# Five groups' expert results by way of DRAM, in a mixer and mixture-of-experts block

## The chip, the cores and the metric

One core of one Trainium2 chip runs the whole program. The metric is the device time in microseconds (us) from start to end of one execution, taken as the median of three runs. The profile shows one further execution of the same program.

## The reference

The block has three stages. RMSNorm and modulation of 512 latent and 256 context tokens of 1,024 elements feed a combined projection, two bidirectional linear recurrences (GLA and retention), a gated merge and an output projection. Then comes the part that the change touches, a hierarchical mixture of experts, and at the end a final RMSNorm:

```python
def hier_moe(h, w_rg, b_rg, w_re, b_re, w_gate, w_up, w_down):
    # top-1 of 4 groups, then top-2 of the 8 experts in it: 512 tokens x 2 = 1,024 rows over 32 experts
    ...
    x_pad = jnp.zeros((P, D), h.dtype).at[dest].set(xt[stok])
    ...
    def expert_block(args):
        xb, e = args
        hid = jax.nn.silu(xb @ w_gate[e]) * (xb @ w_up[e])
        return hid @ w_down[e]
    y = lax.map(expert_block, ...)
    out = jnp.zeros((T, D), jnp.float32).at[tok_pad].add(y.astype(jnp.float32) * w_pad[:, None])

h_lat = h_lat + g2 * hier_moe(modulate(rmsnorm(h_lat, norm_ffn), sh2, sc2), ...)
return rmsnorm(h_lat, norm_final)
```

Everything is fp32. Each expert has a gate, an up (1,024 x 256) and a down matrix (256 x 1,024), 3.1 MB together, about 100 MB for all 32.

## The kernel before

Tokens are put into slots: 14 groups of 128 slots, and each group serves one, two or four experts (2, 2, 4, 1, 4, 1, 2, 4, 1, 2, 4, 1, 2, 2 of them). Which experts share a group follows from how many tokens each one has. The first two groups hold experts whose weights are loaded before the routing is known. `tokG` holds each slot's token, `slotw` its routing weight, `slot` each token's two slot numbers, and `hres[0..3]` the residual stream, 128 tokens each.

Weights come as 192 tiles of 128 x 1,024 (0.5 MB each) in the order of the list `TL`; `feed` (L1108) issues them on SyncE's queue, gate and up at L1124, down at L1127, into a ring of 34 buffers `raw` (L1098). A buffer is handed on when TensorE's matmuls on it are issued (`done_with`). The framework gives each DMA issue one of eight semaphores in turn, in the order of the program text, and an issue waits until the DMA that had its semaphore before has landed.

For each group the main loop (L1476) runs `tokens` (gather of token rows by Pool, transposes on TensorE L1145), `gate_up` (L1158, both products into one PSUM tile, then SiLU on ACT and a product on VectorE), `hidden` (transposes L1174) and `down` in two halves k = 0, 1 (L1185). After the second half `add_results` (L1199) weights the result (`y`, VectorE, L1205), splits it into two parts of reduced precision (`yh` on ACT L1206, `yl` on VectorE L1207), builds a one-hot matrix of the slots' tokens (`hot`, L1209) and appends eight "units" to a list: a unit is two matmuls that spread 128 slots over 128 tokens (L1215) and a VectorE add into `hres` (L1216). The next group's `gate_up` works the units off between its own matmuls, in portions of 0, 2, 3 and 3; what is left is done at the start of the next `add_results`. `y`, `yh` and `yl` have one buffer each. Pools of named tiles, with waits set by the framework, keep everything in order; on each engine instructions run in the order that the framework's scheduler has written.

After the last group `results` (L1427) squares and normalises `hres` and stores the four output tiles (L1438). The routing ahead of the stage (L847 to L893) modulates each 128 tokens on Pool and ACT (L863, L866, L868) and stores them to DRAM as `xf_d`, from which the gathers (L984) read.

Of the kernel before, what the change touches and what calls it, by code (L numbers as in the profile page):

```python
# [11 lines left out]
F32 = mybir.dt.float32  # L12
F32R = mybir.dt.float32r
I32 = mybir.dt.int32
# [28 lines left out]

NE = 11
NR = 8
NB = 8
NL = 7
RING = NE + NR + NB + NL

# [9 lines left out]
NG = len(GROUPS)  # L59

GIVE = (0, 2, 3, 3)
LC = 3
LRJ = 5
PUMP = 5
# [60 lines left out]
def kernel(ctx: ExitStack, tc: tile.TileContext, io, dbg=None):  # L125
# [21 lines left out]
    def pj(shape=(128, 512)):  # L147
        return ps.tile(list(shape), F32, name="pj", bufs=4)
# [655 lines left out]
            feat_block(io[wb][0], 256 * j, (Branch(br, 0), Branch(br, 1)), False, merge(br, j))  # L804


    xf_d = dram.tile([T, D], F32, name="xf_d")

    wr = sb.tile([128, NK, 40], F32, name="wr")
# [145 lines left out]
    tokF, slotw = (sb.tile([128, NG], F32, name=n) for n in ("tokF", "slotw"))  # L955
    ctl = sb.tile([1, 32], I32, name="ctl")
    slot = sb.tile([128, 4, 2], F32, name="slot")
    capr = sb.tile([128, 32], F32, name="capr")
    bno = sb.tile([128, 1], F32, name="bno")
    nc.gpsimd.memset(bno, 0.0)  # L960
# [6 lines left out]
    def ring(kind, n, size, make):  # L967

        r = RINGS.setdefault(kind, {})
        if n % size not in r:  # L970
            r[n % size] = make()
        return r[n % size]

    def w4(name, dt=F32):
        return PM[0].tile([128, D], dt, name=name, tag="w4", bufs=8)
# [78 lines left out]
    def slot_weights():  # L1054

        w, P = RK["ing"], RK["P"]
        nc.vector.tensor_mul(w, w, wk.rearrange("p i k -> p (i k)")[:, :, None].to_broadcast([128, 8, NG]))
        pw = sc((128, NG))
        for m in range(8):
            nc.tensor.matmul(pw, P[:, m].bitcast(F32), w[:, m], start=(m == 0), stop=(m == 7))  # L1060
        nc.vector.tensor_copy(slotw, pw)

    def overflow():

# [114 lines left out]
    def down(g, k):  # L1179
        st, (kind, *es) = EX[g], GROUPS[g]  # L1180
        if k == 0:
            st["p"] = pj(), pj()
        for n2 in range(2):
            for e, r in zip(es, halves(g)):
                nc.tensor.matmul(st["p"][n2][r], st["h"][:, k, r], WT["d", g, k, 0, e][:, 512 * n2:512 * (n2 + 1)],  # L1185
                                 start=(k == 0), stop=(k == 1))
        done_with(len(es))
        if k == 0:
            return
        y, h, l = (ring(n, 0, 1, lambda: w4(n, F32 if n == "y" else F32R)) for n in ("y", "yh", "yl"))  # L1190
        add_results(st["p"], slotw[:, g:g + 1], tokF[:, g:g + 1], y, h, l, one_hot(g % 2))
        del EX[g]

    def one_hot(n):
        if not HT:
            HT[0] = t4([128, 2, 4, 128], "hot", F32R)
        return HT[0][:, n]

    def add_results(p, w, tok, y, h, l, hot):  # L1199

        while units:
            units.pop(0)()
        for n2 in range(2):
            cs = slice(512 * n2, 512 * (n2 + 1))
            nc.vector.scalar_tensor_tensor(y[:, cs], p[n2], w, ada_b[3][:, cs], op0=OP.mult, op1=OP.mult)  # L1205
            nc.scalar.copy(h[:, cs], y[:, cs])  # L1206
            nc.vector.tensor_sub(l[:, cs], y[:, cs], h[:, cs])  # L1207
        for i in range(4):
            nc.vector.tensor_scalar(hot[:, i], iot, 128.0 * i, tok, op0=OP.add, op1=OP.is_equal)  # L1209

        def unit(i, n):
            cs = slice(512 * n, 512 * (n + 1))
            q = sc()
            for m, x in enumerate((h, l)):
                nc.tensor.matmul(q, hot[:, i], x[:, cs], start=(m == 0), stop=(m == 1))  # L1215
            nc.vector.tensor_add(hres[i][:, cs], hres[i][:, cs], q)  # L1216

        units.extend(partial(unit, i, n) for i in range(4) for n in range(2))

    raws, staged = {}, {}  # L1220
# [122 lines left out]
    def overflow_block(po):  # L1343

        def t4(shape, name, dt=F32):
            big = math.prod(shape[1:]) == D
            return po.tile(shape, dt, name=name, tag="b4" if big else name, bufs=6 if big else 1)
# [67 lines left out]
        for n2 in range(2):  # L1415
# [4 lines left out]
            for k in range(2):  # L1420
                nc.tensor.matmul(p, hT[:, k], w[:, k], start=(k == 0), stop=(k == 1))
            ps2.append(p)
        add_results(ps2, ow, otok, t4([128, D], "y"), t4([128, D], "yh", F32R), t4([128, D], "yl", F32R), one_hot(0))
        while units:
            units.pop(0)()

# [49 lines left out]
    for g in range(NG + 1):  # L1476
        early = g == len(PAIR_EARLY)
        if early:
            down(g - 1, 0)
            down(g - 1, 1)  # L1480
        if g < NG:
            gate_up(g)
            if g + 2 < NG:
                tokens(g + 2)
        if g and not early:
            down(g - 1, 0)
        if g < NG:
            hidden(g)
        if g and not early:
            down(g - 1, 1)  # L1490
        if g == 0:
            slot_weights()
        if g == 3:
            extra = overflow()
        if g == NG - 1:

            free = -(-(len(TL) - NE - NR - NB) // RING) * RING + NE + NR + NB
            nfin = raw_tile(free)
            nc.sync.dma_start(nfin, bass.AP(tensor=io["norm_final"].tensor, offset=io["norm_final"].offset,
                                            ap=[[0, 128], [1, D]]))  # L1500

            with tc.issue_after(last["hT"].ins):
                nc.scalar.activation(small(1, "va"), eps, AF.Sqrt)
# [31 lines left out]
```

## Time and profile before

| | |
|---|---|
| time, median of 3 runs | 1128.74 us (1125.59 to 1130.0) |
| profiled execution, own time | 1129.64 us |
| its span | 1127.8 us |
| TensorE busy | 1026.6 us (91%) |
| VectorE, ACT, Pool busy | 609.4 (54%), 344.1 (31%), 262.6 us (23%) |
| granted TensorE clock, mean | 0.963 of full speed |
| read from DRAM, written | 188.44 MB, 4.19 MB |
| share of the chain that ended last | TensorE 50%, VectorE 5%, DMA 1% |

The page cuts the span into 40 slices of 28.2 us. The expert stage takes the last ten, from about 846 us:

```profile
PE   3989899899999999999999999999729999999993
...
DMA  9860212332223302433442251448179999999801
GB/s 304 207 206 20 67 38 85 94 96 54 76 64 106 112 26 72 140 102 79 129 149 75 75 168 56 131 146 339 48 264 385 407 407 408 407 408 407 329 1 76
```

In the first two rows a digit is the busy share of a slice in tenths; the third is what the DMA engines moved. TensorE is busy in both long stages; the DMA engines are full in the expert stage alone.

### The profile page before, as it was taken

How to read it: one execution, taken by the hardware profiler on the slowest of the kernel's cores; microseconds unless marked ns; L12 is line 12 of the kernel's file. 1: busy time of each engine (PE TensorE's matmuls, PEld its weight loads, DVE VectorE, ACT ScalarE, POOL GpSimd, SP SyncE). 2: the span in 40 equal slices, each digit the busy share in tenths (PEclk: the TensorE clock that was granted, in tenths of full speed). 3: DMA queues.
4: the chain of work that ended last, by engine and by line, in shares of the span. 5: the costliest groups of instructions: out<-in, count | busy, mean ns of one | idle time of the engine just before them, and what ended most of it. 6: DMA issues, size and time to landing. Idle time of an engine off the chain costs nothing.

```text
span 1127.8 us, 17400 instructions
## 1 busy us (share of the span) xinstructions
PE 1026.6 (91%) x6726; PEld 837.9 (74%) x6726; DVE 609.4 (54%) x1113; ACT 344.1 (31%) x594; POOL 262.6 (23%) x316
## 2 busy tenths in 40 slices
PE   3989899899999999999999999999729999999993
PEld 1779888799898988999887888889726655554542
DVE  4546677877688444534544241463352655454556
ACT  4237345455443222122233132333321111111012
POOL 0014234443726142414230100121431000000001
PEclk9999899999999999999999999999759999999997
DMA  9860212332223302433442251448179999999801
GB/s 304 207 206 20 67 38 85 94 96 54 76 64 106 112 26 72 140 102 79 129 149 75 75 168 56 131 146 339 48 264 385 407 407 408 407 408 407 329 1 76
DMA packets 105773, 190.66 MB, mean 169 GB/s; under 512 B 10882, under 2 KB 72660, under 8 KB 105688
## 3 DMA queue, kind: packets, MB, share of 16 engines
q1 hardware_dynamic: 98968, 180.53, 46.9%
q10 hardware_dynamic: 4576, 4.78, 1.4%
q0 software_dynamic: 2144, 4.21, 1.0%
q8 instruction: 54, 0.88, 0.3%
q14 instruction: 31, 0.25, 0.1%
HBM read 188.44 MB, written 4.19 MB: 171 GB/s over the span
## 4 chain that ended last, share of the span: by engine, by line
PE 50%; DVE 5%; DMA 1%; issue 1%; ACT 1%; POOL 0%; SPq 0%; ACTq 0%; DVEq 0%; POOLq 0%
PE pj L341 16%; PE pj L1158 10%; PE pj L332 9%; PE sc L1215 5%; PE pj L1185 4%; PE sc L1145 1%; DMA xg<-xf_d,tokG 1%; DVE y L1205 1%; PE sc L862 1%; DVE hres L1216 1%; DVE wl L1243 0%; DVE qs L594 0%; PE sc L1174 0%; ACT yh L1206 0%; PE sc L755 0%
## 5 line engine op out<-in xcount | busy, mean ns | idle before, releaser
L332 PE MATMUL pj<-wh,xh 128*128 128x256 f32 x800 | 229.7, 287 | 3.6 <-ACT wh L1238 2.3
L332 PE MATMUL pj<-wh,xl 128*128 128x256 f32 x800 | 227.4, 284 | 0.0
L332 PE MATMUL pj<-wl,xh 128*128 128x256 f32 x800 | 227.1, 284 | 0.0
L1243 DVE TENSOR_TENSOR wl<-raw,wh 128x1024 fp32r<-128x1024 f32 x88 | 118.6, 1355 | 100.6 <-ACT wh L1238 53.2
L332 PEld LDWEIGHTS pj<-wh,xh 128*128 128x128 f32 x800 | 153.9, 192 | 4.7 <-ACT wh L1238 2.5
L332 PEld LDWEIGHTS pj<-wh,xl 128*128 128x128 f32 x800 | 153.0, 191 | 0.7
L332 PEld LDWEIGHTS pj<-wl,xh 128*128 128x128 f32 x800 | 152.4, 191 | 0.2
L1238 ACT CAST wh<-raw 128x1024 fp32r<-128x1024 f32 x88 | 91.5, 1048 | 170.0 <-PE pj L332 44.2
L1158 PE MATMUL pj<-raw,xt 128*32 128x256 f32 (+2 forms) x1024 | 118.2, 383 | 0.0
L1158 PEld LDWEIGHTS pj<-raw,xt 128*32 128x32 f32 (+2 forms) x1024 | 69.6, 130 | 40.3 <-issue 9.6
L1216 DVE TENSOR_TENSOR hres<-hres,sc 128x512 f32<-128x512 f32 x112 | 71.0, 683 | 39.6 <-PE sc L1215 39.6
L341 PE MATMUL pj<-xh,wh 128*128 128x512 f32 (+1 forms) x216 | 82.8, 388 | 3.3 <-ACT wh L1238 3.2
L341 PE MATMUL pj<-xl,wh 128*128 128x512 f32 (+1 forms) x216 | 82.8, 385 | 0.0
L341 PE MATMUL pj<-xh,wl 128*128 128x512 f32 (+1 forms) x216 | 82.5, 382 | 0.0
L341 PE MATMUL pj<-oT,wh 128*128 128x512 f32 x256 | 81.7, 399 | 0.8 <-ACT oT L760 0.5
L703 DVE SCALAR_TENSOR_TENSOR adaacc<-wada,scT,adaacc 128x1024 f32<-128x1024 f32 x28 | 39.3, 1403 | 41.9 <-DMA wada<-in_w_ada 41.9
L1215 PE MATMUL sc<-yh,hot 128*128 128x512 f32 x112 | 50.4, 457 | 9.4 <-ACT yh L1206 9.0
L341 PEld LDWEIGHTS pj<-oT,wh 128*128 128x128 f32 x256 | 48.2, 191 | 12.6 <-ACT oT L760 1.0
L1185 PE MATMUL pj<-raw,hT 128*32 128x512 f32 (+2 forms) x256 | 53.6, 600 | 0.0
L341 PE MATMUL pj<-oT,wl 128*128 128x512 f32 x128 | 50.3, 395 | 0.0
L1215 PE MATMUL sc<-yl,hot 128*128 128x512 f32 x112 | 47.9, 437 | 2.5 <-DVE yl L1207 2.4
L341 PEld LDWEIGHTS pj<-xh,wh 128*128 128x128 f32 x216 | 40.7, 190 | 11.0 <-ACT wh L1238 3.3
(380 smaller groups left out, 1796.1 us busy)
## 6 DMA issues: line engine op xcount, KB each, us to landing
raw<-in_w_in SPq DMA_DIRECT2D x64, 512.0 KB
raw<-in_w_expert_up SPq DMA_DIRECT2D x64, 512.0 KB
raw<-in_w_expert_gate SPq DMA_DIRECT2D x64, 512.0 KB
raw<-in_w_expert_down SPq DMA_DIRECT2D x64, 512.0 KB
wada<-in_w_ada SPq DMA_DIRECT2D x32, 512.0 KB
wada<-in_w_ada SPq DMA_DIRECT2D x32, 256.0 KB
raw<-in_w_branch_gla SPq DMA_DIRECT2D x8, 512.0 KB
raw<-in_w_branch_ret SPq DMA_DIRECT2D x8, 512.0 KB
```

The source lines that it names most:

```text
L332: nc.tensor.matmul(out, x, (wh, wl)[wi][:, k], start=(start and first and k == 0 and n == 0), stop=(a == 1 and k == 3 and n == 2), skip_gr ...
L341: nc.tensor.matmul(out, (wh, wl)[wi][:, k, 128 * f:128 * (f + 1)], (th, tl)[xi][kk], start=(start and first and k == 0 and n == 0), stop=( ...
L703: nc.vector.scalar_tensor_tensor(a, w, s, a, op0=OP.mult, op1=OP.add)
L862: nc.tensor.matmul(pl, hT[:, kk], wr[:, kk], start=(kk == 0), stop=(kk == NK - 1))
L1145: nc.tensor.transpose(p[:, k], xg(g)[:, 128 * kk:128 * (kk + 1)], ident)
L1158: nc.tensor.matmul(p[r, u], st["x"][:, 4 * a + k, r], WT["gu", g, a, u, e][:, k], start=(a == 0 and u == 0 and k == 0), stop=(a == 1 and k ...
L1185: nc.tensor.matmul(st["p"][n2][r], st["h"][:, k, r], WT["d", g, k, 0, e][:, 512 * n2:512 * (n2 + 1)], start=(k == 0), stop=(k == 1))
L1205: nc.vector.scalar_tensor_tensor(y[:, cs], p[n2], w, ada_b[3][:, cs], op0=OP.mult, op1=OP.mult)
L1215: nc.tensor.matmul(q, hot[:, i], x[:, cs], start=(m == 0), stop=(m == 1))
L1216: nc.vector.tensor_add(hres[i][:, cs], hres[i][:, cs], q)
L1238: nc.scalar.copy(parts[0], raw)
L1243: return nc.vector.tensor_sub(l, raws.pop(n), h)
```

## The change

The results of groups 0 to 4 are not spread by one-hot matmuls. VectorE weights them as before (now L1215), ACT's queue stores the 128 x 1,024 tile `y` to a DRAM tile `ys_d` at the group's slots (L1216), and no `yh`, `yl`, `hot` and units are made. In the loop's turns 6 to 9 a new function `fetch` takes up one `hres` tile each: for the two experts of each token Pool clears a tile `row`, gathers rows of `ys_d` by the token's slot number (`rowI`; a slot number of 640 or more is skipped and leaves zeros) and adds the tile into `hres` on Pool. The two `row` tiles take the place of two buffers of the weight ring, which goes from 34 to 32. The one-hot matrix of groups 5 to 13 is made at the first half of `down` (`mark`). The last group has `yh` and `yl` tiles of its own, and its parts are computed ahead of what is left of group 12's units. Line numbers after the change are higher by 3 to 33.

```diff
--- before.py
+++ after.py
@@ -43,7 +43,7 @@
 
 NE = 11
 NR = 8
-NB = 8
+NB = 6
 NL = 7
 RING = NE + NR + NB + NL
 
@@ -59,6 +59,9 @@
 NG = len(GROUPS)
 
 GIVE = (0, 2, 3, 3)
+
+LAST = 9
+MID = NG - LAST
 LC = 3
 LRJ = 5
 PUMP = 5
@@ -804,6 +807,7 @@
             feat_block(io[wb][0], 256 * j, (Branch(br, 0), Branch(br, 1)), False, merge(br, j))
 
 
+    ys_d = dram.tile([128 * MID, D], F32, name="ys_d")
     xf_d = dram.tile([T, D], F32, name="xf_d")
 
     wr = sb.tile([128, NK, 40], F32, name="wr")
@@ -955,6 +959,7 @@
     tokF, slotw = (sb.tile([128, NG], F32, name=n) for n in ("tokF", "slotw"))
     ctl = sb.tile([1, 32], I32, name="ctl")
     slot = sb.tile([128, 4, 2], F32, name="slot")
+    rowI = sb.tile([128, 8], I32, name="rowI")
     capr = sb.tile([128, 32], F32, name="capr")
     bno = sb.tile([128, 1], F32, name="bno")
     nc.gpsimd.memset(bno, 0.0)
@@ -1059,6 +1064,18 @@
         for m in range(8):
             nc.tensor.matmul(pw, P[:, m].bitcast(F32), w[:, m], start=(m == 0), stop=(m == 7))
         nc.vector.tensor_copy(slotw, pw)
+        nc.gpsimd.tensor_copy(rowI, slot.rearrange("p i k -> p (i k)"))
+
+    def fetch(i):
+
+        h, rows = hres[i], []
+        for m in range(2):
+            b = ring("row", m, 2, lambda: PB[0].tile([128, D], F32, name="row", tag="mb2", bufs=2))
+            nc.gpsimd.memset(b, 0.0)
+            gather(b, rowI[:, 2 * i + m:2 * i + m + 1], 128 * MID, ys_d)
+            rows.append(b)
+        for b in rows:
+            nc.gpsimd.tensor_add(h, h, b)
 
     def overflow():
 
@@ -1180,6 +1197,8 @@
         st, (kind, *es) = EX[g], GROUPS[g]
         if k == 0:
             st["p"] = pj(), pj()
+            if g >= MID:
+                mark(one_hot(g % 2), tokF[:, g:g + 1])
         for n2 in range(2):
             for e, r in zip(es, halves(g)):
                 nc.tensor.matmul(st["p"][n2][r], st["h"][:, k, r], WT["d", g, k, 0, e][:, 512 * n2:512 * (n2 + 1)],
@@ -1187,8 +1206,16 @@
         done_with(len(es))
         if k == 0:
             return
-        y, h, l = (ring(n, 0, 1, lambda: w4(n, F32 if n == "y" else F32R)) for n in ("y", "yh", "yl"))
-        add_results(st["p"], slotw[:, g:g + 1], tokF[:, g:g + 1], y, h, l, one_hot(g % 2))
+        y = ring("y", 0, 1, lambda: w4("y"))
+
+        h, l = (ring(n, g // (NG - 1), 2, lambda: w4(n, F32R)) for n in ("yh", "yl"))
+        if g < MID:
+            for n2 in range(2):
+                cs = slice(512 * n2, 512 * (n2 + 1))
+                nc.vector.scalar_tensor_tensor(y[:, cs], st["p"][n2], slotw[:, g:g + 1], ada_b[3][:, cs], op0=OP.mult, op1=OP.mult)
+            nc.scalar.dma_start(ys_d[128 * g:128 * g + 128], y)
+        else:
+            add_results(st["p"], slotw[:, g:g + 1], y, h, l, one_hot(g % 2), g == NG - 1)
         del EX[g]
 
     def one_hot(n):
@@ -1196,18 +1223,21 @@
             HT[0] = t4([128, 2, 4, 128], "hot", F32R)
         return HT[0][:, n]
 
-    def add_results(p, w, tok, y, h, l, hot):
-
-        while units:
-            units.pop(0)()
+    def mark(hot, tok):
+        for i in range(4):
+            nc.vector.tensor_scalar(hot[:, i], iot, 128.0 * i, tok, op0=OP.add, op1=OP.is_equal)
+
+    def add_results(p, w, y, h, l, hot, apart=False):
+
+        rest, units[:] = list(units), []
+        if not apart:
+            while rest:
+                rest.pop(0)()
         for n2 in range(2):
             cs = slice(512 * n2, 512 * (n2 + 1))
             nc.vector.scalar_tensor_tensor(y[:, cs], p[n2], w, ada_b[3][:, cs], op0=OP.mult, op1=OP.mult)
             nc.scalar.copy(h[:, cs], y[:, cs])
             nc.vector.tensor_sub(l[:, cs], y[:, cs], h[:, cs])
-        for i in range(4):
-            nc.vector.tensor_scalar(hot[:, i], iot, 128.0 * i, tok, op0=OP.add, op1=OP.is_equal)
-
         def unit(i, n):
             cs = slice(512 * n, 512 * (n + 1))
             q = sc()
@@ -1215,6 +1245,7 @@
                 nc.tensor.matmul(q, hot[:, i], x[:, cs], start=(m == 0), stop=(m == 1))
             nc.vector.tensor_add(hres[i][:, cs], hres[i][:, cs], q)
 
+        units.extend(rest)
         units.extend(partial(unit, i, n) for i in range(4) for n in range(2))
 
     raws, staged = {}, {}
@@ -1420,7 +1451,8 @@
             for k in range(2):
                 nc.tensor.matmul(p, hT[:, k], w[:, k], start=(k == 0), stop=(k == 1))
             ps2.append(p)
-        add_results(ps2, ow, otok, t4([128, D], "y"), t4([128, D], "yh", F32R), t4([128, D], "yl", F32R), one_hot(0))
+        mark(one_hot(0), otok)
+        add_results(ps2, ow, t4([128, D], "y"), t4([128, D], "yh", F32R), t4([128, D], "yl", F32R), one_hot(0))
         while units:
             units.pop(0)()
 
@@ -1492,6 +1524,8 @@
             slot_weights()
         if g == 3:
             extra = overflow()
+        if MID < g <= MID + 4:
+            fetch(g - MID - 1)
         if g == NG - 1:
 
             free = -(-(len(TL) - NE - NR - NB) // RING) * RING + NE + NR + NB
```

SyncE's queue, first part of the expert stage: weights of the single-expert group 3 (gate and up), the eight down tiles of group 2, and the first of group 4. The number in DMAHW is the semaphore that an issue takes and waits for; register instructions in between are left out. Before:

```order
L1124 DMA raw<-in_w_expert_gate 128x1024 [waits DMAHW5_49,PE_49]
...
L1124 DMA raw<-in_w_expert_up 128x1024 [waits DMAHW6_49,PE_49]
...
L1127 DMA raw<-in_w_expert_down 128x1024 [waits DMAHW7_49,PE_49]
...
L1127 DMA raw<-in_w_expert_down 128x1024 [waits DMAHW0_49,PE_49]
...
L1127 DMA raw<-in_w_expert_down 128x1024 [waits DMAHW1_49,PE_49]
...
L1127 DMA raw<-in_w_expert_down 128x1024 [waits DMAHW2_49,PE_49]
```

After, on the same queue, and then the stores on ACT's:

```order
L1141 DMA raw<-in_w_expert_gate 128x1024 [waits DMAHW5_49,PE_49]
...
L1141 DMA raw<-in_w_expert_up 128x1024 [waits DMAHW7_49,PE_49]
...
L1144 DMA raw<-in_w_expert_down 128x1024 [waits DMAHW0_49,PE_49]
...
L1144 DMA raw<-in_w_expert_down 128x1024 [waits DMAHW1_49,PE_49]
...
L1144 DMA raw<-in_w_expert_down 128x1024 [waits DMAHW3_49,PE_49]
...
L1144 DMA raw<-in_w_expert_down 128x1024 [waits DMAHW4_49,PE_49]
...
L1144 DMA raw<-in_w_expert_down 128x1024 [waits DMAHW5_49,PE_49]
...
L1144 DMA raw<-in_w_expert_down 128x1024 [waits DMAHW6_49,PE_49]
```

```order
L1193 COPY hT<-sc 128x256 [waits PE_49]
L1216 DMA ys_d<-y 128x1024 [waits DMAHW6_49,DVE_49]
L1216 DMA ys_d<-y 128x1024 [waits DMAHW2_49,DVE_49]
L1183 ACTIVATE hid<-pj 128x256 [waits PE_49]
```

Semaphores 6 and 2 are missing from the weights' row: the first store has taken 6 and the second 2. The next weight on 6, the sixth of the eight down tiles, waits for the first store.

Pool, from the modulation of the last token tiles (`xf`, `xfp`) to the end. Before:

```order
L863 TENSOR_TENSOR xf<-hres,adab_174 128x1024
L868 TENSOR_TENSOR xfp<-xfp,shp 128x1024
L1033 TENSOR_TENSOR wr<-cge 128x112
L1034 TENSOR_TENSOR oj<-wr,tok_183 128x112
L984 DMA xg<-xf_d,tokG 128x1024 x14
L1434 TENSOR_TENSOR raw<-hres,raw 128x1024 x2
```

After:

```order
L1074 MEMSET row 128x1024 x2
L867 TENSOR_TENSOR xf<-hres,adab_174 128x1024
L872 TENSOR_TENSOR xfp<-xfp,shp 128x1024
L1067 CAST rowI<-slot 128x8
L1038 TENSOR_TENSOR wr<-cge 128x112
L1039 TENSOR_TENSOR oj<-wr,tok_184 128x112
L989 DMA xg<-xf_d,tokG 128x1024 x12
L989 DMA row<-ys_d,rowI 128x1024 x2
L1078 TENSOR_TENSOR hres<-hres,row 128x1024
L1074 MEMSET row 128x1024
L1078 TENSOR_TENSOR hres<-hres,row 128x1024
L989 DMA row<-ys_d,rowI 128x1024
```

Two memsets stand ahead of the last token tile's modulation, and the fetches follow the twelfth token gather; the last two token gathers come among them.

VectorE, from the last group's SiLU product `hid` to the end of the expert stage. Before:

```order
L1167 TENSOR_TENSOR hid<-hid,pj 128x256
L1205 SCALAR_TENSOR_TENSOR y<-pj,slotw,adab_175 128x512 x2
L1207 TENSOR_TENSOR yl<-y,yh 128x512 x2
L1216 TENSOR_TENSOR hres<-hres,sc 128x512 x3
L1205 SCALAR_TENSOR_TENSOR y<-pj,slotw,adab_175 128x512
L1216 TENSOR_TENSOR hres<-hres,sc 128x512 x5
L1207 TENSOR_TENSOR yl<-y,yh 128x512
L1205 SCALAR_TENSOR_TENSOR y<-pj,slotw,adab_175 128x512
L1216 TENSOR_TENSOR hres<-hres,sc 128x512
L1207 TENSOR_TENSOR yl<-y,yh 128x512
L1216 TENSOR_TENSOR hres<-hres,sc 128x512 x7
```

After:

```order
L1184 TENSOR_TENSOR hid<-hid,pj 128x256
L1238 SCALAR_TENSOR_TENSOR y<-pj,slotw,adab_175 128x512 x2
L1240 TENSOR_TENSOR yl<-y,yh 128x512 x2
L1246 TENSOR_TENSOR hres<-hres,sc 128x512 x3
L1238 SCALAR_TENSOR_TENSOR y<-pj,slotw,adab_175 128x512 x2
L1246 TENSOR_TENSOR hres<-hres,sc 128x512
L1240 TENSOR_TENSOR yl<-y,yh 128x512 x2
L1246 TENSOR_TENSOR hres<-hres,sc 128x512 x12
```

The last group's two halves of `y` and `yl` now stand ahead of the last twelve adds.

## Rows read from the trace of the kernel before

**Rows 1.** Stretches: us, busy time by engine (instructions), granted clock, DMA share, GB/s.
```profile
860.00:880.00 20.00, 20.00 (x129) 11.12 (x129) 10.26 (x25) 2.58 (x5) 0.99 (x1) 1.00 1.03 411
...
1066.00:1080.00 14.00, 13.63 (x73) 6.65 (x69) 5.27 (x10) 1.99 (x4) 0.00 (x0) 1.00 0.06 24
```

**Rows 2.** SyncE queue's waits, 880 to 1066: total us, times, longest.
```profile
SPq L1124 <- DMA raw<-in_w_expert_up: 21.4, 28, 1.9
```

**Rows 3.** Timeline of SyncE's queue: start, us to the last's end, issues; down weights.
```profile
948.53 4.19 SPq L1127 DMA_DIRECT2D raw<-in_w_expert_down  x4
...
959.73 9.65 SPq L1127 DMA_DIRECT2D raw<-in_w_expert_down  x8
...
1005.62 4.17 SPq L1127 DMA_DIRECT2D raw<-in_w_expert_down  x4
...
1015.84 9.30 SPq L1127 DMA_DIRECT2D raw<-in_w_expert_down  x8
```

**Rows 4.** Timeline of TensorE: the second down halves of groups 6 and 9.
```profile
978.03 1.94 PE L1185 MATMUL pj<-raw,hT 128*64 128x512 f32 x8
...
1036.44 1.94 PE L1185 MATMUL pj<-raw,hT 128*64 128x512 f32 x8
```

**Rows 5.** Groups by line, 820 to 1128: count, busy us, mean ns, idle before.
```profile
L1215 PE MATMUL sc<-yh,hot 128*128 128x512 f32 x112 | 50.4, 457 | 9.4 <-ACT yh L1206 9.0
L1215 PE MATMUL sc<-yl,hot 128*128 128x512 f32 x112 | 47.9, 437 | 2.5 <-DVE yl L1207 2.4
```

**Rows 6.** Timeline of TensorE: scatter matmuls one behind another.
```profile
877.10 0.39 PE L1215 MATMUL sc<-yl,hot 128*128 128x512 f32 x1
...
879.42 0.39 PE L1215 MATMUL sc<-yl,hot 128*128 128x512 f32 x1
```

**Rows 7.** Timeline of VectorE: y of groups 0 and 1.
```profile
872.61 1.61 DVE L1205 SCALAR_TENSOR_TENSOR y<-pj,slotw,adab 128x512 f32<-128x512 f32 x2 [2.59 <-PE pj L1185]
...
876.04 1.61 DVE L1205 SCALAR_TENSOR_TENSOR y<-pj,slotw,adab 128x512 f32<-128x512 f32 x2 [0.45 <-PE pj L1185]
```

**Rows 8.** Timeline of SyncE's queue: group 2's down weights, group 4's up weights.
```profile
864.43 7.66 SPq L1127 DMA_DIRECT2D raw<-in_w_expert_down  x8
...
878.46 5.59 SPq L1124 DMA_DIRECT2D raw<-in_w_expert_up  x4
```

**Rows 9.** Pool's queue (packets, MB); gathers' landing; the output stores' first and last start.
```profile
q0 software_dynamic: 2144, 4.21, 1.0%
...
DMA to landing us min/median/max: 4.9/7.4/9.7
...
L1438 SPq DMA_DIRECT2D out<-raw x4: 332/336/349, 1117.3 to 1121.9; - x4
```

**Rows 10.** Timeline of VectorE: y of groups 4 and 5.
```profile
940.71 1.41 DVE L1205 SCALAR_TENSOR_TENSOR y<-pj,slotw,adab 128x512 f32<-128x512 f32 x2 [2.84 <-PE pj L1185]
...
959.36 0.75 DVE L1205 SCALAR_TENSOR_TENSOR y<-pj,slotw,adab 128x512 f32<-128x512 f32 x1 [1.97 <-PE pj L1185]
```

**Rows 11.** Pool's and ACT's timelines, last token tile; tile view of the clearing memsets.
```profile
817.60 2.35 POOL L863 TENSOR_TENSOR xf<-hres,adab 128x1024 f32<-128x1024 f32 x1 [1.42 <-PE sc L857]
...
821.00 2.11 ACT L866 ACTIVATE xfp<-xf,xfry 128x1024 f32<-128x1024 f32 x1 [0.28 <-DVE xfry L185]
...
L1468 POOL MEMSET xg<- x3: 952/952/953, 806.5 to 808.3; 128x1024 f32 x3
```

**Rows 12.** Timeline of VectorE: from the last group's y to the last add.
```profile
1101.04 0.75 DVE L1205 SCALAR_TENSOR_TENSOR y<-pj,slotw,adab 128x512 f32<-128x512 f32 x1 [1.32 <-PE pj L1185]
...
1108.51 0.69 DVE L1216 TENSOR_TENSOR hres<-hres,sc 128x512 f32<-128x512 f32 x1 [1.02 <-PE sc L1215]
1109.37 3.68 DVE L1216 TENSOR_TENSOR hres<-hres,sc 128x512 f32<-128x512 f32 x6 [0.17 <-PE sc L1215]
```

**Rows 13.** TensorE's timeline at its wait near 1056, and the stretch after it.
```profile
1057.46 0.50 PE L1215 MATMUL sc<-yh,hot 128*128 128x512 f32 x1 [1.63 <-ACT yh L1206]
...
1060.00:1062.00 2.00, 2.00 (x6) 1.23 (x4) 1.43 (x3) 0.00 (x0) 0.00 (x0) 0.52 1.02 408
```

## The prediction

> **What bounds the kernel now.** I read the table of stretches first, then SyncE's waits and its timeline, then TensorE's timeline. In the expert stage the reader is to see two engines full at once: TensorE is busy in all of 860 to 880, and the DMA engines show a share of 1.03 at 411 GB/s there; from 1066 on the DMA share is 0.06, so the stage ends with TensorE and VectorE alone [rows 1]. SyncE issues a weight transfer only when an earlier one has landed: its largest wait in 880 to 1066 is for a weight transfer, 28 times [rows 2]. In a run of eight issues the step is (9.30 - 0.33)/7 = 1.28 us, or (9.65 - 0.33)/7 = 1.33 [rows 3], which is 0.524 MB at 411 GB/s or a little less. Each issue waits for the one eight places before it, so the landing of transfer n is the issue of n+8. That gives the number on which this case turns, the lead of the weights over their use. Group 6's last weight tile is the fourth of the four issued from 948.53; eight places later stands the fourth of the row at 959.73, so it landed at 959.73 + 3 x 1.33 = 963.7. TensorE uses it at 978.03 [rows 3, 4]: a lead of 14.3 us. For group 9 it is 1015.84 + 3 x 1.28 = 1019.7 against 1036.44, 16.8 us. TensorE is the bound, but with only some 14 us between it and the DMA engines.
>
> **The change, part by part.**
>
> *Scatter taken from TensorE.* Groups 0 to 4 lose 5 of 14 sets of one-hot products, 80 of the 224 matmuls. They follow one another at (879.42 - 877.10)/10 = 0.232 us [rows 6], so 18.6 us; and the waits for the two halves in front of them are 9.4 + 2.5 = 11.9 us in all [rows 5], 5/14 of which is 4.2. TensorE alone would gain 22.8 us. That is more than the lead: before group 6 its own saving would run TensorE into weights that have not landed. The gain is what is left of the lead after the change has delayed the weights.
>
> *Bytes of the five stores.* Each is 0.524 MB in a stretch that is full, so five weight slots of 1.28 us: 6.4 us of delay, all before group 6's weights.
>
> *Bytes of the fetches.* All 14 gathers of tokens carried 4.21 MB [rows 9], which is 1,024 rows. Groups 0 to 4 hold 13 of 32 experts, so about 416 of the rows, 1.70 MB or 4.2 us over the four fetches, if tokens spread evenly; at most 640 rows, 6.4 us. Two of the four come before group 6's last weights: 2.1 us, at most 3.2.
>
> *Stores in SyncE's cycle.* The order of the changed program shows that ACT's stores take places in the same cycle of eight. Store 0 takes one ahead of group 2's down weights, and the sixth of those eight (of the row at 864.43, issued at 864.43 + 5 x 1.05 = 869.7 before [rows 8]) then waits for store 0. The two products of y(0) end at 872.61 + 1.61 = 874.2 [rows 7], so that weight is issued 4.5 us late and more, by the time L that the store takes. What stands behind it on SyncE is every later weight. In front of it the fifth landed when the first "up" of the row at 878.46 was issued, and the store's 1.3 us follow, so the DMA engines are dry from 879.8. The late weight lands at 874.3 + L + 4.9 (4.9 us is the shortest landing of a gather of at most the same size [rows 9]) instead of 881.1: idle time of L - 1.9. Since y has one buffer, y(1) (876.04 before) also waits for store 0; store 1 leaves at 874.3 + L + 1.6, and four weights later one waits for it: a second idle time of L - 4.8. For stores 2 to 4 more than 15 us lie between the store and the weight that waits for it, and I count nothing.
>
> The trace shows no store under load, so L has bounds. From below 4.9, the shortest gather under full weights. From above 10.2, a weight transfer behind its fellows (8 x 1.28). Between them the last `out` store, of the same size on idle queues: issued at 1121.9, and the span ends at 1127.8, so at most 5.9 [rows 9]. I take 5.4, the middle of the two nearest rows: idle 3.5 + 0.6 = 4.1 us.
>
> *A rule against the row.* The gathers on Pool's queue landed in 4.9 to 9.7 us beside a weight queue that takes over 10 [rows 9], so another queue is not simply served last. The Trainium skill (DMA: Bandwidth & Descriptors, Queues, rings and completion order) says that each DMA engine takes turns between the queues that have work; by that alone a store would need two weight slots, 2.6 us, the idle time would be 0.7 and the sum 6.2 us faster. The same page (Anatomy of one DMA) holds that the confirmation of the write is most of a transfer's fixed cost and slowest where the target is HBM, which is this store's case and speaks for the larger L. No run here shows either yet.
>
> *Pool.* Two memsets of 0.95 us now stand ahead of the last token row's modulation on Pool [rows 11]. Pool waited 1.42 us there until 817.60; ACT takes the result at 821.00, and 817.60 + 2.35 = 819.95 leaves 1.05 us more. Hidden; if the cover were gone, 0.5 to 1.9. The adds into `hres` cost 2.35 each on Pool and must follow store 4: y(4) was at 940.71, y(5) at 959.36 [rows 10]. Store 4 lands near 944, two gathers of 4.9 to 7.4 us and two adds end near 956 to 959, when group 5's first products want `hres[0]`: up to 3 us of wait. TensorE has 22.8 us in hand against weights there, so it costs nothing before group 6; the other three fetches have a group's time each.
>
> *The ring.* Two buffers fewer move two early weights only; SyncE waits for landings, not buffers, in the full stretch [rows 2]. Nothing, at most 0.5.
>
> *Last group.* VectorE's chain from y(13) at 1101.04 to the last of the adds at 1109.37 + 3.68 = 1113.05 is 12.0 us with gaps of 1.02 and 0.17 [rows 12]. With tiles of its own the last group's halves are ready before group 12's remaining products are through, and the gaps close: 1.1 us, on the path.
>
> *Sum.* At group 6: lead 14.3 - stores 6.4 - idle 4.1 - two fetches 2.1 = 1.7. At group 9: 16.8 - 6.4 - 4.1 - 4.2 = 2.1. After that the weights are early (nothing moves from 1066 on), so TensorE keeps the smaller, 1.7. With the tail 1.1: 2.8 us faster, 1126.8 against the profiled execution's own 1129.64 (its span 1127.8 and 1.8 around it). That execution lies 0.9 over the median of the three runs, so the same kernel would read 1125.9 in their terms.
>
> **The rivals.**
>
> *A, the forecast: the DMA engines become the bound and eat nearly all.* L from 4.9 to 5.9 gives 3.8 to 1.8 faster; the lead is read to one slot (1.3), and the larger fetch takes 1.1 more. From 5.1 faster to 0.6 slower: 1123.6 to 1129.3. Chance 0.45.
>
> *B, the transfers cost less.* If the stores leave no idle time, the sum is 14.3 - 6.4 - 2.1 + 1.1 = 6.9 faster, 1121.8; if the added bytes find room as well, the lead alone decides, 14.3 + 1.1 = 15.4, 1113.3. For it: gathers under load landed in half the weights' time. Against: the DMA share is already 1.03. Chance 0.25.
>
> *C, slower: SyncE stands behind late stores.* One mechanism, at one of group 2's and one of group 4's weights, with L - 1.9 + L - 4.8 of idle time. It decides from the L at which this reaches 6.9, that is 6.8 us. At the gathers' median of 7.4 the idle is 8.1 and the kernel 1.2 slower, 1129.9; at 9.7 it is 5.8, 1134.5; at 10.2, 6.8, 1135.5. For it: stores arrive into a full DMA queue. Against: the idle-queue store of 5.9. Chance 0.22.
>
> *D, the clock.* After TensorE's wait of 1.63 us before 1057.46 the granted clock was 0.52 in 1060 to 1062, the lower of its two levels, 1.2 GHz, for nearly all of it [rows 13]: 1.0 us lost in these two. TensorE will now wait for some 20 us in all. Falls before group 9 are hidden by the next wait for weights; three behind it would cost 3, and the result is 1128.9. Chance 0.08.
>
> **How the numbers follow.** The predicted time is A's, 1125.9. The range has to take in B's nearer half and most of C: 1116 to 1134. A's own range is 1123.6 to 1129.3. What a measurement of this kernel can tell from no change is 0.5%, 5.6 us: 1123.1 and 1134.4. Faster than the first: most of B (0.23) and the lower end of A (0.12), 0.35. Slower than the second: the upper quarter of C and a little for what I have not seen, 0.14. The rest, 0.51, is no change that can be measured.
>
> **What would show it.** In the changed profile TensorE should wait in 880 to 1036 for weight transfers, some 15 to 20 us in all, where it now hardly waits; SyncE should show one wait of 8 to 11 us near 870 to 880 for store 0, and the GB/s a dip there; the scatter should count 144 matmuls; VectorE should have no gap from y(13) to its last add. Store landings under 4 us or weights that keep their lead mean B; over 7 us, C. I am wrong altogether if TensorE waits for `hres` or its banks rather than for weights, or if DMA bandwidth with stores in it falls below some 400 GB/s.

## The result, and the profile after

The changed kernel takes 1134.56 us (median of seven runs, 1131.9 to 1139.49) against 1126.54 for the kernel before in the same comparison: a ratio of 1.0058, with a 95% interval of 1.0037 to 1.0078. It is slower by 6.5 us on 1126.5 (4.2 to 8.8); here and below the ratio is not the plain quotient of the two medians, which is 1.0071 here. I had forecast 2.8 us faster, with 1134 as the upper end of the range.

The profiled execution spans 1132.3 us. These are the first stretches of the expert stage after the change (us; busy time of TensorE, its weight loads, VectorE, ACT and Pool, each with the number of instructions; granted clock, DMA share, GB/s):

```profile
846.00:860.00 14.00, 13.74 (x102) 9.51 (x102) 2.50 (x4) 2.52 (x5) 2.97 (x3) 0.85 0.75 246
860.00:880.00 20.00, 20.00 (x184) 10.46 (x187) 4.92 (x16) 1.34 (x3) 0.99 (x1) 1.00 1.00 401
880.00:900.00 20.00, 17.18 (x149) 11.00 (x138) 5.14 (x8) 2.69 (x6) 1.98 (x2) 1.00 0.73 247
900.00:920.00 20.00, 13.13 (x124) 6.15 (x128) 0.00 (x0) 0.59 (x1) 0.99 (x1) 0.91 1.02 408
920.00:940.00 20.00, 19.23 (x102) 11.38 (x90) 3.63 (x6) 2.10 (x5) 1.98 (x2) 1.00 0.99 381
940.00:960.00 20.00, 15.81 (x81) 7.06 (x81) 4.92 (x7) 2.58 (x5) 3.58 (x3) 1.00 0.99 368
```

and of the kernel before:

```profile
846.00:860.00 14.00, 13.30 (x99) 9.63 (x99) 2.49 (x4) 2.51 (x5) 2.97 (x3) 0.85 0.95 358
...
880.00:900.00 20.00, 20.00 (x186) 13.76 (x185) 11.25 (x25) 2.48 (x5) 0.99 (x1) 1.00 1.03 407
```

The last number of each row is the one to read. Before, the DMA engines were full from 860 on (407 or 408 GB/s in each stretch of 20 us from 880 to 980). Now there are holes: 358 to 246 GB/s in 846 to 860 is 3.8 us of full rate lost, 407 to 247 in 880 to 900 is 7.9, and 381 and 368 in the two stretches from 920, against 408 and 407, are 1.3 and 1.9. TensorE, busy in all of 880 to 940 before, has holes from 880 on.

Who holds the weights stands in SyncE's waits, 860 to 1100 (total us, times, longest):

```profile
SPq L1144 <- DMA ys_d<-y: 21.3, 3, 8.3
...
SPq L1141 <- DMA ys_d<-y: 7.5, 1, 7.5
```

and when, in the timelines of ACT's queue (four of the five stores) and of SyncE's (the weights; each row begins with the first issue's start and the us to the last one's end):

```profile
873.42 9.75 ACTq L1216 DMA_DIRECT2D ys_d<-y  x2
...
925.55 0.33 ACTq L1216 DMA_DIRECT2D ys_d<-y  x1
...
943.28 0.33 ACTq L1216 DMA_DIRECT2D ys_d<-y  x1
```

```profile
881.39 1.48 SPq L1144 DMA_DIRECT2D raw<-in_w_expert_down  x3
...
892.32 1.88 SPq L1141 DMA_DIRECT2D raw<-in_w_expert_gate  x2
...
932.44 0.33 SPq L1144 DMA_DIRECT2D raw<-in_w_expert_down  x1
...
950.56 0.33 SPq L1144 DMA_DIRECT2D raw<-in_w_expert_down  x1
```

Store 0 is issued at 873.42 and store 1 at 873.42 + 9.75 - 0.33 = 882.84. The weights that wait for them go at 881.39 and 892.32, 0.1 us after the landings that the semaphore events give, so the stores took 7.9 and 9.4 us; stores 3 and 4 took 6.8 and 7.2 by the same reading. Each of these four weights waited 6.5 to 8.3 us, and every later weight with it. Store 2, issued at 897.07, took 7.9 us and held nothing up: SyncE was by then so late that the weight on its semaphore, at 905.41, followed the issue before it by 0.6 us.

At the other end of the chain, TensorE now waits for weights (840 to 1110; before, no wait for weights stood in this list):

```profile
...
PE pj L1175 <- DMA raw<-in_w_expert_gate: 9.5, 9, 2.8
PE pj L1175 <- DMA raw<-in_w_expert_up: 6.1, 10, 0.7
PE sc L1245 <- ACT yh L1239: 5.5, 4, 1.7
...
PE pj L1204 <- DMA raw<-in_w_expert_down: 1.3, 1, 1.3
PE sc L1245 <- DVE hres L1246: 0.3, 1, 0.3
```

TensorE's rows at the two places of [rows 4]:

```profile
985.74 2.60 PE L1204 MATMUL pj<-raw,hT 128*64 128x512 f32 x5
...
1043.69 1.94 PE L1204 MATMUL pj<-raw,hT 128*64 128x512 f32 x8
```

985.74 against 978.03 and 1043.69 against 1036.44: 7.7 and 7.3 us late. The semaphore events of the trace put the landing of group 6's last weight at 987.7 and of group 9's at 1043.6, where they were 963.8 and 1019.6: 23.9 and 24.0 us late. The lead of 14.3 is spent and more.

The tail did gain. VectorE from the last group's y to the last add:

```profile
1106.76 1.41 DVE L1238 SCALAR_TENSOR_TENSOR y<-pj,slotw,adab 128x512 f32<-128x512 f32 x2 [1.32 <-PE pj L1204]
1108.09 0.67 DVE L1246 TENSOR_TENSOR hres<-hres,sc 128x512 f32<-128x512 f32 x1
1108.68 1.28 DVE L1240 TENSOR_TENSOR yl<-y,yh 128x512 fp32r<-128x512 f32 x2
1109.88 7.25 DVE L1246 TENSOR_TENSOR hres<-hres,sc 128x512 f32<-128x512 f32 x12
```

It ends at 1117.13, 10.4 us after its start, without a gap; before it was 12.0 [rows 12].

### The profile page after: what moved, and what is told of

Read it like the earlier page. It is cut to its first block, busy times and chain, and to the rows that moved or that the text cites. A ratio compares the mean times of both kernels' runs of the same rounds, so it can differ in the third digit from the quotient of the medians.

```text
span 1132.3 us, 17212 instructions
## 1 busy us (share of the span) xinstructions
PE 1013.8 (90%) x6646; PEld 821.5 (73%) x6646; DVE 577.0 (51%) x1043; ACT 338.6 (30%) x584; POOL 297.4 (26%) x341
## 3 DMA queue, kind: packets, MB, share of 16 engines
q0 software_dynamic: 3296, 5.99, 1.5%
## 5 line engine op out<-in xcount | busy, mean ns | idle before, releaser
L1175 PE MATMUL pj<-raw,xt 128*32 128x256 f32 (+2 forms) x1024 | 124.0, 387 | 15.6 <-DMA raw<-in_w_expert_gate 9.5
L1204 PE MATMUL pj<-raw,hT 128*32 128x512 f32 (+2 forms) x256 | 59.9, 600 | 1.3 <-DMA raw<-in_w_expert_down 1.3
L1246 DVE TENSOR_TENSOR hres<-hres,sc 128x512 f32<-128x512 f32 x72 | 45.5, 682 | 23.6 <-PE sc L1245 21.1
L426 POOL TENSOR_TENSOR th<-th,g 128x512 f32<-128x512 f32 x16 | 25.4, 1613 | 86.1 <-ACT th L425 83.7
L344 PEld LDWEIGHTS pj<-xl,wh 128*128 128x128 f32 x216 | 41.1, 190 | 8.1 <-DVE xl L318 0.4
```

Of the source, the lines that this page charges most:

```text
L344: nc.tensor.matmul(out, (wh, wl)[wi][:, k, 128 * f:128 * (f + 1)], (th, tl)[xi][kk], start=(start and first and k == 0 and n == 0), stop=( ...
L426: nc.gpsimd.tensor_mul(th, th, g)
L1175: nc.tensor.matmul(p[r, u], st["x"][:, 4 * a + k, r], WT["gu", g, a, u, e][:, k], start=(a == 0 and u == 0 and k == 0), stop=(a == 1 and k ...
```

## The experiments

Ratios are against the kernel before, run on the same chip in the same comparison, with 95% intervals; 0.1% is 1.1 us. Medians of different comparisons differ by some 4 us for the same kernel, and the expert stage began between 841 and 852 us in the profiled executions, so ratios and times within a trace are compared, not spans. Where landings of two traces are compared, they are counted from the first token transposes, called the stage's start here (846.08 in the kernel before, 844.90 in the changed one).

My theory after the result (T): SyncE's weight queue is held by the stores' landings. The rivals: the bytes (U), Pool's adds and the waits for `hres` (W), the smaller ring (V).

**The stores on Pool's queue.**

```diff
-            nc.scalar.dma_start(ys_d[128 * g:128 * g + 128], y)
+            nc.gpsimd.dma_start(ys_d[128 * g:128 * g + 128], y)
```

> Only the queue of the five stores differs from the changed kernel: Pool's instead of ACT's, the same bytes. Theory T (SyncE's weight queue is held: a store takes a place in the cycle of eight semaphores that SyncE's weights use, lands 7 to 9 us after its issue, and the weight with the same semaphore and every later one waits): group 6's last weight, 23.9 us late in the changed kernel, is late by the bytes of stores (6.4), of two fetches (2.1) and the smaller ring (3.6), 12 us; the lead of 14.3 leaves 2.2, the tail adds 1.1: 3.3 faster than before, about 1123.2. Rival U (the bytes themselves, or writes to DRAM that slow the weights): unchanged, 1133 to 1136. Rival W (Pool's adds or the fetches hold VectorE and TensorE): unchanged too, with TensorE waiting for hres rather than for weights.

Ratio 0.9967 (0.9941 to 0.9994): 0.9% or 10 us faster than the changed kernel, with the same bytes. The holes from 880 on are gone and SyncE waits for no store, though each store still takes 6.9 to 8.5 us (stretches as above):

```profile
846.00:860.00 14.00, 13.64 (x113) 9.82 (x114) 3.58 (x11) 1.93 (x4) 2.97 (x3) 0.94 0.86 302
880.00:900.00 20.00, 20.00 (x192) 12.81 (x180) 5.05 (x8) 2.87 (x7) 4.26 (x5) 1.00 1.03 410
900.00:920.00 20.00, 14.91 (x94) 8.38 (x94) 2.52 (x4) 1.16 (x3) 0.57 (x1) 1.00 1.03 410
920.00:940.00 20.00, 16.21 (x95) 7.78 (x93) 2.62 (x4) 1.93 (x4) 2.79 (x4) 1.00 1.03 410
```

410 GB/s with stores in it is as much as before, so a store costs its own bytes and no more. Group 6's last weight lands at 974.7, 10.9 us late, or 12.8 from the stage's start, where T said 12. U falls as the main cause, and so does W.

**No stores and no fetches.**

```diff
-            nc.scalar.dma_start(ys_d[128 * g:128 * g + 128], y)
...
-        if MID < g <= MID + 4:
-            fetch(g - MID - 1)
```

> Leaves out the stores and the fetches, so the results of groups 0 to 4 are missing from the output; all else as in the changed kernel (ring of 32, last group's own tiles). T: weights late only by the ring's 3.6; the lead of 14.3 leaves 10.7, tail 1.1: 11.8 faster than before, about 1114.7, TensorE's own saving (22.8) is not reached since weights cap it. U: the same to within 3 us. If the loss came from the rest of the change (TensorE's order, the ring, the memsets), it stays at 1126 or above.

Ratio 0.9912 (0.9879 to 0.9945), 9.9 us, within the forecast's reach. The rest of the change is a gain, and even without any transfer of its own it is capped by weights: TensorE waits 8.0 + 1.4 us for them, and in the profile it begins group 6's second half at 966.95, 11.1 us earlier than before (9.8 from the stage's start), where the last weight landed at 967.2.

**The last group's own tiles alone.**

```diff
-NB = 6
+NB = 8
...
-LAST = 9
+LAST = NG
...
-        if MID < g <= MID + 4:
-            fetch(g - MID - 1)
```

> Only the last group's own tiles, its parts ahead of group 12's remaining units, and the one-hot built at the first half of down; no store, no fetch, ring of 34. T: the tail's 1.1 us alone, about 1125.4, VectorE without a gap from the last y to the last add. Rival: nothing, 1126.5, because the wait moves to another place of the tail; or 1 slower if the earlier one-hot delays a y.

Ratio 0.998 (0.9956 to 1.0003): 2.3 us with an interval that holds my 1.1, the 1.6 that the tail shows, and zero. In the profile the chain from y to the last add is 10.4 us, as in the changed kernel. The size is not settled by the time, only by the trace.

**The ring's first 34 weights as before.**

```diff
+    def borrowed(m):
+        return ring("row", m, 2, lambda: PB[0].tile([128, D], F32, name="row", tag="mb2", bufs=2))
...
     def raw_tile(m):
+        if m in (RING, RING + 1):
+            return borrowed(m - RING)
...
-        feed(used[0] + RING)
+        feed(used[0] + RING + (2 if used[0] < RING else 0))
```

> The changed kernel, but the two row buffers first serve once as weight buffers 33 and 34, so that the first 34 weights are issued as before the change. T: the weights' delay before store 0 (3.6 us in the traces) goes and every later weight comes 3.6 earlier or, where SyncE waits for a store which itself follows TensorE, only in part: 1131 to 1134. Rival V (the smaller ring is the main cause): 1127 or less. U and W: unchanged, 1134.5.

Ratio 1.0033 (1.0009 to 1.0056): between T's two ends, 2.8 us better than the changed kernel, though the two intervals overlap. In the trace group 6's last weight lands 140.2 us after the stage's start, against 142.8 in the changed kernel: 2.6 us earlier. V falls as the main cause.

**Tiny stores, no fetches.**

```diff
-            nc.scalar.dma_start(ys_d[128 * g:128 * g + 128], y)
+            nc.scalar.dma_start(ys_d[128 * g:128 * g + 128, 0:16], y[:, 0:16])
...
-            fetch(g - MID - 1)
```

> Leaves out the fetches, and each of the five stores on ACT's queue writes 16 of 1,024 columns (8 KB): the results of groups 0 to 4 are missing from the output. The semaphores of the cycle are taken as in the changed kernel; bytes and landing time are taken away. T: a small store lands some 2.5 us after its issue, the weight that waits for it is issued while eight are still queued, so as without any store: ratio about 0.990, 11 us faster than before. Rival X (a store in the cycle costs whatever its size, since its issue is late): 1.000 or more. In between, a small write to DRAM takes 5 us or more to land: 0.995.

Ratio 0.9955 (0.993 to 0.998): the case in between. A store of 8 KB still took 5.3 to 6.4 us by the semaphores. The first left at 875.98 and the weight behind it at 882.54 (ACT's queue, SyncE's queue, and the stretch):

```profile
875.98 7.68 ACTq L1216 DMA_DIRECT2D ys_d<-y  x2
...
882.54 0.33 SPq L1144 DMA_DIRECT2D raw<-in_w_expert_down  x1
...
880.00:900.00 20.00, 20.00 (x216) 13.13 (x212) 4.68 (x8) 2.69 (x6) 1.98 (x2) 1.00 0.77 269
```

269 GB/s with almost no bytes of its own: the hole is a wait, not traffic. It is about 5 us of time against no stores at all, and the intervals of the two overlap. The trace's records of single packets show where a small store's time goes: 3.1 to 3.5 us from the issue to its first packet, 1.4 to 1.9 to the end of its last, 0.4 to 1.0 more to the landing. In the changed kernel the full stores took 3.4 to 4.1, 2.9 to 5.1 and 0.3 to 0.4 us. Two stores of 0.5 MB in the kernel before (`xf_d`, SyncE's queue, issued at 790.65 and 800.53, in a slice of 48 GB/s) had their first packet after 0.8 us and landed after 2.6 and 2.7. So over half of a small store's time is gone before its first packet moves; why the first packet comes so late is open.

**A second buffer for y.**

```diff
-NB = 6
+NB = 5
...
-        y = ring("y", 0, 1, lambda: w4("y"))
+        y = ring("y", g % 2 if g < MID else 0, 2, lambda: w4("y") if g >= MID or g % 2 == 0 else PB[0].tile([128, D], F32, name="y2", tag="y2", bufs=1))
```

> The changed kernel with a second buffer for y in groups 0 to 4 (ring of 31 instead of 32), so that y(1) and store 1 do not wait for store 0. T: store 1 leaves near 877 instead of 882.8, its weight (issued at 892.3 in the changed kernel) near 885; the weights come 5 us earlier, less 1.8 for the ring; later stores hold them as before: ratio 1.002 to 1.004, against 1.0058. If the single buffer of y was no part of it: 1.006 or more.

Ratio 1.0005 (0.9982 to 1.0027), 6 us better than the changed kernel and somewhat more than I expected. The two stores now leave 3.4 us apart (880.09 and 883.52) instead of 9.4, so they share one hole instead of digging two: the weight behind the second goes out without a wait of its own.

**Pool's queue and the ring's first 34 weights together.** The edits of the first and the fourth experiment.

> Stores on Pool's queue, and the two row buffers serve once as weight buffers 33 and 34. T: the weights, 10.9 us late at group 6 with the stores on Pool's queue alone, come 3.6 earlier; lead 14.3 leaves 7.0, tail 1.7, less 1.2 because the first token gathers stand behind two more weights: 7.5 faster than before, ratio 0.993 (stores on Pool's queue alone: 0.9967). If the ring does nothing: 0.9967.

Ratio 0.9956 (0.9932 to 0.9979), against 0.9967 for Pool's queue alone: a miss, since 0.993 was expected and no gain beyond the intervals is seen. From the stage's start (first token transposes, at 848.17 and 844.25) the 34th weight lands 4.1 us earlier, but group 2's fifth down weight (the 49th) only 1.0: after the loan the ring is full, and weights wait for TensorE's use instead. Group 6's last weight comes 1.4 us earlier. What I had called the ring's 3.6 us is not to be had back whole by two early buffers.

**Three groups by DRAM.** The same with one constant.

```diff
-LAST = 9
+LAST = 11
```

> As the one with Pool's queue and borrowed buffers, but only three groups (0 to 2, 8 of 32 experts) go by DRAM. T: the bound is the weights, so fewer bytes gain more than TensorE's smaller saving (3/5 of 22.8 = 13.7) loses: weights late by 3 x 1.28 + 2.6 = 6.4, or 7.5 less, lead leaves 7 to 8, tail 1.7, start -1.2: ratio 0.992 to 0.993. If TensorE is the bound after all: 0.996, since 9 us of its saving are gone.

Ratio 0.9912 (0.9882 to 0.9941), 9.9 us faster than the kernel before and 1.5% faster than the changed kernel. Less work taken from TensorE gives more than five groups in the experiment before (0.9956; the two intervals overlap a little), since the weights are later by less: TensorE's waits (840 to 1110) now hold 3.6 us for weights, where with five groups they held 7.2 + 1.4:

```profile
...
PE sc L1252 <- ACT yh L1246: 8.1, 5, 1.7
PE pj L1182 <- DMA raw<-in_w_expert_up: 3.6, 4, 1.8
PE sc L1252 <- DVE hres L1253: 1.5, 2, 1.2
```

**The ring of 32 alone**, in the kernel before.

```diff
-NB = 8
+NB = 6
```

> The kernel before with the ring of 32 instead of 34 and nothing else. T: weights 33 and 34 are issued some 12 us later, the weights after them land 2 to 4 us later, and the lead (10.9 us at group 4's up weights, 14.3 at group 6) covers it: ratio 0.998 to 1.002, no wait of TensorE for weights. If the smaller ring cost time by itself: 1.003 or more.

Ratio 0.9999 (0.998 to 1.0018), and no wait of TensorE for weights in its list. By itself the smaller ring is free; it only takes from the lead: group 6's last weight lands 122.4 us after the stage's start, 117.7 in the kernel before, so it takes 4.7 us of that lead.

**Two groups by DRAM.** As the one with three, `LAST = 12`.

> Pool's queue, borrowed buffers, two groups (0 and 1, 4 of 32 experts) by DRAM. T: TensorE's saving is 2/5 of 22.8 = 9.1; stores 2.6 and fetches 1.3 delay the weights by 3.9 and the ring by 2 to 3: the lead leaves 7.5, tail 1.7: ratio 0.992, TensorE waiting for weights no more than 2 us in all. If the time follows TensorE's saving alone: between three groups' 0.9912 and the last group's tiles alone (0.998), 0.994.

Ratio 0.9977 (0.9959 to 0.9995): a miss, and both explanations of mine missed its cause. TensorE's waits show no weights, but `hres`:

```profile
...
PE sc L1252 <- ACT yh L1246: 8.1, 5, 1.7
PE sc L1252 <- DVE hres L1253: 6.8, 3, 5.3
```

The longest stands at 903 to 908 (TensorE, VectorE, Pool; idle time and releaser in brackets):

```profile
908.54 0.79 PE L1252 MATMUL sc<-yh,hot 128*128 128x512 f32 x1 [5.34 <-DVE hres L1253]
...
907.80 3.08 DVE L1253 TENSOR_TENSOR hres<-hres,sc 128x512 f32<-128x512 f32 x5 [6.82 <-POOL hres L1078]
...
901.36 2.36 POOL L1078 TENSOR_TENSOR hres<-hres,row 128x1024 f32<-128x1024 f32 x1 [3.23 <-DMA row<-ys_d,rowI]
...
905.43 2.34 POOL L1078 TENSOR_TENSOR hres<-hres,row 128x1024 f32<-128x1024 f32 x1 [0.70 <-DMA row<-ys_d,rowI]
```

Read from below: Pool waits for the gathered rows, VectorE's first add into `hres[0]` waits for Pool, the four PSUM buffers of the scatter fill up, and TensorE waits. This is rival W. In the changed kernel it is hidden (0.3 us of wait for `hres`), since TensorE is late with weights anyway.

**Two groups, fetched two turns later.**

```diff
-        if MID < g <= MID + 4:
-            fetch(g - MID - 1)
+        if MID + 2 < g <= MID + 6:
+            fetch(g - MID - 3)
```

> Two groups by DRAM over Pool's queue with borrowed buffers, as the one that gave 0.9977, but each fetch two groups later in the loop (turns 5 to 8 instead of 3 to 6). There TensorE waited 6.8 us for hres, 5.3 of it at 903 to 908, where VectorE's first add of group 2 stood behind Pool's two adds of the first fetch. If that wait ate the gain: it goes, and the ratio is 0.991 to 0.993. If the two groups' saving is just smaller than reckoned: 0.997 again. If the wait moves to a later fetch: 0.995 or more, with TensorE waiting for hres in 920 to 990.

Ratio 0.9925 (0.9896 to 0.9954), and 1.4 us of wait for `hres` is left of the 6.8. The two intervals do not meet: the early fetch ate most of the two groups' gain.

**No fetches, stores on ACT's queue.**

```diff
-        if MID < g <= MID + 4:
-            fetch(g - MID - 1)
```

> The changed kernel with the five stores on ACT's queue but without fetches (the results of groups 0 to 4 are missing from the output). T: SyncE is held by all five stores as in the changed kernel; only the fetches' bytes go, 1.7 MB or 4 us in front of group 9's weights, 2 in front of group 6's: ratio 1.002 to 1.004. Rival W (Pool's clears and adds, or waits for hres): 0.997 or less.

Ratio 1.0028 (1.0006 to 1.005), as T had it. SyncE waits for the stores as in the changed kernel, 21.5 us in three waits and 7.8 in one:

```profile
SPq L1144 <- DMA ys_d<-y: 21.5, 3, 9.5
...
SPq L1141 <- DMA ys_d<-y: 7.8, 1, 7.8
```

Against the changed kernel the fetches cost 0.3% or 3.4 us, near the 4.2 of their bytes, though the two intervals overlap.

## Why the prediction was wrong

**What bounds the kernel: right.** The weights' lead of 14 us caps the gain. TensorE's saving of 22.8 us did not show with no transfer at all (9.9 us). In the changed kernel TensorE waits 9.5 + 6.1 + 1.3 = 16.9 us for weights, as the prediction said it would (15 to 20).

**Stores in SyncE's cycle: the step that failed.** The mechanism was rival C's and had its place right, but the forecast rested on two numbers that were wrong; the ring's, below, is the third. First, L: I took 5.4 us, between a gather at 4.9 and an idle-queue store at 5.9, and C needed 6.8. The stores took 6.8 to 9.4. The gathers' median of 7.4 in the same row [rows 9] was the better neighbour: transfers of at most the same size under the same load. The 5.9 was no more than a bound, as the prediction says: by the semaphore events the four `out` stores landed in 2.6 to 3.1 us, so the load, and not the size, makes L. With the 7.4 my formula gives 8.1 us of idle time at stores 0 and 1 instead of 4.1, and the GB/s lost 7.9 in 880 to 900. That agreement has some luck in it: with the measured 7.9 and 9.4 the formula gives 6.0 + 4.6 = 10.6, but the two late weights landed 3.8 and 3.4 us after their issues where I had 4.9. Second, "for stores 2 to 4 more than 15 us lie between the store and the weight that waits for it, and I count nothing" has the order reversed. SyncE runs up to a ring ahead of TensorE, so the weight that takes the store's semaphore next would be issued before the store: for store 3 at 911.2 in the trace before, while y(3) ended at 925.8. Stores 3 and 4 therefore hold SyncE too, not the first two alone, and in 920 to 960 that cost 1.3 + 1.9 = 3.2 us more; store 2 found SyncE already late enough and cost nothing.

**The ring: wrong.** I said "nothing, at most 0.5". The two weights were issued 12 us later, and 846 to 860 lost 3.8 us of DMA time. From the stage's start the smaller ring alone makes group 6's last weight 4.7 us late. My reason, that SyncE waits for landings, not buffers, was read from rows that begin at 880, and the ring decides before that. Alone it costs no time (0.9999), but the change had already spent the lead that would have covered it.

**The ledger.** Forecast for group 6's last weight: 6.4 + 4.1 + 2.1 = 12.6 us late. Measured: 23.9. The stretches add to it: bytes 6.4 + 2.1, the first hole 7.9, the later two 3.2, the ring 3.8, and 0.5 in 860 to 880 (401 GB/s): 23.9. So exact a sum is partly luck, since the stage began 1.2 us earlier here and part of the third fetch fell into this time too. Counted from the stage's start the weight is 25.1 late: the ring's 4.7, the bytes' 8.5, and 11.9 left over, where the holes from 860 on add up to 11.6. The lead of 14.2 leaves 9.7 us to be lost, of which 7.7 show at the first matmul of that half, since the last weight is used a little behind it. The last group's y is 5.7 late and the tail returns 1.6. From group 9, 7.3 late, to that y 1.6 us come back; that is about the clock, which in the kernel before fell to 0.63 in 1058 to 1060 and 0.52 in 1060 to 1062 [rows 13], 1.7 us lost, and stood at 1.00 in both in the changed kernel's profile.

**Bytes: right.** With Pool's queue the weights were 12.8 late from the stage's start, and 6.4 + 2.1 and the ring's 4.7 make 13.2. The 1.7 MB of the fetches are 5.99 - 4.21 = 1.78 MB on Pool's queue.

**Pool and `hres`: right for this kernel**, for the reason given (TensorE has time in hand against weights). With two groups, where no wait for weights is left, the wait for `hres` came to 6.8 us.

**The tail: right,** 1.6 us where I had 1.1.

**Rivals B and D.** B's condition, stores that land in under 4 us, did not occur. D's clock falls hardly took place: the granted clock was 0.91 in 900 to 920, where TensorE was busy for 13.13 of 20 us, and in 960 to 980, and 1.00 (the upper of its two levels, 2.4 GHz) in the other stretches of 20 us from 860 to 1100.

**The rule weighed.** The Trainium skill's turn-taking between queues (DMA: Bandwidth & Descriptors, Queues, rings and completion order), by which I estimated 2.6 us for a store, bears on one part of the time alone: the packets of the five stores were on the move for 2.9 to 5.1 us, and another 3.4 to 4.1 had passed before the first. The Trainium skill's sentence (DMA: Bandwidth & Descriptors, Anatomy of one DMA, which describes transfers issued by Pool) that the confirmation of the write dominates a transfer's fixed cost and is slowest towards HBM is not borne out as the reason here: from the end of the last packet to the landing the stores on ACT's queue took 0.3 to 0.4 us, the small ones 0.4 to 1.0. Whether a packet's recorded end holds part of the confirmation, no run shows.

## What to carry to other kernels

Where DMA issues take semaphores in turn, a new transfer on any of those queues becomes a link in the chain of the others: find the next issue with the same semaphore and ask whether it goes out before the new transfer can have landed. Putting the store on a queue outside the cycle was worth 10 us here with not a byte changed. And where two engines are both nearly full, work moved from one to the other paid here only up to the lead between them: three groups moved gave 9.9 us, two 8.5 once they were fetched later, five 5.0 at best (0.9912, 0.9925, 0.9956).

## What was not expected of the hardware

A store to DRAM of 0.5 MB took 6.8 to 9.4 us beside a full weight queue on ACT's queue and 6.9 to 8.5 on Pool's, and one of 8 KB 5.3 to 6.4. On ACT's queue 3.4 to 4.1 us of it passed before the first packet of a full store and 3.1 to 3.5 before that of a small one; a weight on SyncE's queue, issued at 881.39 when that queue had run empty, had its first packet after 1.0 us. Reads and stores together kept 410 GB/s, the same as reads alone.
